# Routing by halves of a row and a first quad gathered from the token tiles, in a two-layer MoE trunk

## The chip, the cores and the metric

The kernel runs on one core of a Trainium2 chip. The metric is the device time of one execution, in microseconds (us); smaller is better. The engines are PE (TensorE, the matmul engine; PEld is its weight load), DVE (VectorE), ACT (ScalarE), POOL (GpSimd) and SP (SyncE, which here does nothing but issue the weight loads).

## What is computed

A decoder trunk of two layers on 528 tokens (16 meta tokens and 512 others) of 1024 columns, in float32. Each layer has a mixer (layer 0: a gated short convolution, layer 1: attention), an output projection added to the stream `h`, and a hierarchical mixture of experts (MoE). The MoE is what the change is about: 8 groups of 8 experts, each token goes to the group with the highest logit and there to two experts.

```python
def hier_moe(hn, w_grp, w_exp, w_gate, w_up, w_down):
    ...
    g_logits = (xf @ w_grp).astype(jnp.float32)
    p_grp = jax.nn.softmax(g_logits, axis=-1)
    grp = jnp.argmax(g_logits, axis=-1).astype(jnp.int32)
    ...
    e_in = jnp.einsum('ng,nge->ne', jax.nn.one_hot(grp, N_GROUPS, dtype=jnp.float32), e_logits)
    top_p, top_i = lax.top_k(jax.nn.softmax(e_in, axis=-1), TOP_K_IN_GROUP)
    gate = p_g * top_p / jnp.sum(top_p, axis=-1, keepdims=True)
    ...
    def expert_block(args):
        xb, e = args
        hh = jax.nn.silu(xb @ w_gate[e]) * (xb @ w_up[e])
        return hh @ w_down[e]
```

Here `hn` is the normalised stream (each row of `h` times its `rstd`, one over its root mean square, times a gain per column).

## The kernel before

**Tiles.** The tokens lie in four tiles of 128 rows, `h[0]` to `h[3]`, and in layer 0 a fifth of 16 rows, `hm` (index META). In layer 1 the meta tokens are gone and there are four tiles.

**Out-projection and routing.** `project_out` multiplies by the output weights in two halves of 512 columns. In each half the matmuls of all tiles (L292, three each for a split into a high and a low part) go into one PSUM bank per tile, `acc`, of which five are used in turn; as the last step of a half reaches a tile, VectorE adds its bank to `h` (L294). Only after the second half is `done(t)` called, which is `route(t)`: ScalarE squares and sums the row of 1024 columns, GpSimd makes `rstd`; TensorE transposes the tile in two lots of four (L372) through one PSUM bank, `tp`, ScalarE copies the first lot to `hT` (L375) and VectorE the second to `xT1` (L377); eight logit matmuls (L380) go into the PSUM bank `misc`, of which there is one, so the next tile's logits wait until this tile's have been read. Then a chain of some fourteen small VectorE instructions on 128x8 and 128x64 numbers finds the group and the two experts: `gm` (L383), `oh`, `mg`, `se` (L395), `s8`, `eq`, `gt`, `r8`, `M` (L403). `rank(t)` counts with a triangular matmul (L417) which place each token has in its expert and in its group: `rm` (L418), from it the one-hot `d` of places in group 0 (L419) and `aux` (L421); matmuls with ones (L422, L425) carry the counts to the tiles not yet ranked.

**First gather.** `first_gather` takes the tokens of group 0 out of the tiles: per tile one matmul for `aux` (L467) and two of 128x512 for `h` (L431), with `d` as the stationary operand; after the last tile VectorE copies `ag` (L473), ScalarE scales the gathered rows to `xg` (L436, two halves), VectorE makes `sel`, the places within the first four experts (L441), and TensorE selects and transposes them in one go, eight matmuls (L450) into two banks that VectorE multiplies by the gain into `xT0` and `xT1` (L451).

**Quads.** `run` then works through 16 quads of four experts: two `gate_up` passes (L589: all gate weights, then all up weights; PSUM bank `gu`), Silu and product, a transpose (L601), selection of the next quad's tokens, `down` (L621). Two quads share a group's gathered rows, so every second quad calls `gather(g)`: `d` for all tiles in one VectorE instruction, the `aux` matmuls (L561), the `h` matmuls (L431), `ag`, `xg`. In quad 0 the chain `gates` (L489 to L515) runs on VectorE and ScalarE beside the first matmuls, and five short matmuls (L744) after `down` fetch the gates of group 0.

**Order and buffers.** On TensorE the quads run in the order in which they are written. Out-projection and routing are ordered by the tile framework's scheduler, each engine getting a fixed list. The weights, 1 MB a tile, come in one fixed order through a ring of 22 buffers in the MoE stages (rings A, B and R). A load is issued (L101, SP) as soon as a buffer's last matmul is over, that is at the end of a `gate_up` pass or of `down`.

## Time and profile before

| | |
|---|---|
| median of three runs | 1403.22 us (1399.02, 1403.29, 1403.22) |
| profiled execution, its time | 1402.26 us |
| profiled execution, its span | 1400.5 us |
| mean granted TensorE clock | 0.958 |
| PE busy | 1245.6 us (89%) |
| DVE busy | 514.5 us (37%) |
| ACT busy | 310.4 us (22%) |
| weights and other data read | 434.40 MB |

The page cuts the span into 40 slices of 35 us, and gives for each the busy share of each engine in tenths, the granted TensorE clock and the share in which the 16 DMA engines move data. The busy share of TensorE is an average over stages with different limits, so stages are read one by one below: busy time by stretch, then single instructions in order of time. A line of a timeline is a run of like instructions on one engine; what stands in square brackets is the idle time before it and whose end ended that.

### The profile page before, as it was taken

How to read it: one execution, taken by the hardware profiler on the slowest of the kernel's cores; microseconds unless marked ns; L12 is line 12 of the kernel's file. 1: busy time of each engine (PE TensorE's matmuls, PEld its weight loads, DVE VectorE, ACT ScalarE, POOL GpSimd, SP SyncE). 2: the span in 40 equal slices, each digit the busy share in tenths (PEclk: the TensorE clock that was granted, in tenths of full speed). 3: DMA queues.
4: the chain of work that ended last, by engine and by line, in shares of the span. 5: the costliest groups of instructions: out<-in, count | busy, mean ns of one | idle time of the engine just before them, and what ended most of it. 6: DMA issues, size and time to landing. Idle time of an engine off the chain costs nothing.

```text
span 1400.5 us, 22937 instructions
## 1 busy us (share of the span) xinstructions
PE 1245.6 (89%) x9647; PEld 792.7 (57%) x9647; DVE 514.5 (37%) x1238; ACT 310.4 (22%) x708; POOL 58.6 (4%) x146
## 2 busy tenths in 40 slices
PE   8999999999889798878779999999997787888875
PEld 7999866545444343434378888875543334434432
DVE  5555336132131221423436676562230212113135
ACT  6333122011011010121044775331111010101112
POOL 2111101000000000000021000010000000000001
PEclk9999999999999999989989999999999999999998
DMA  7422563899999999999710012959999999999994
GB/s 282 151 91 91 211 249 151 367 420 419 420 419 419 420 420 419 419 421 421 306 42 28 30 63 84 367 219 382 420 420 420 420 419 420 420 419 420 420 418 168
DMA packets 65956, 438.13 MB, mean 313 GB/s; under 512 B 7457, under 2 KB 7841, under 8 KB 15282
## 3 DMA queue, kind: packets, MB, share of 16 engines
q1 hardware_dynamic: 64432, 434.74, 76.1%
q10 hardware_dynamic: 1154, 1.78, 0.4%
q8 instruction: 81, 1.33, 0.4%
q14 instruction: 33, 0.27, 0.1%
q0 software_dynamic: 256, 0.01, 0.0%
HBM read 434.40 MB, written 2.10 MB: 312 GB/s over the span
## 4 chain that ended last, share of the span: by engine, by line
DMA 26%; PE 20%; DVE 2%; ACT 1%; issue 1%; POOL 0%; DVEq 0%; ACTq 0%; SPq 0%; POOLq 0%
DMA R<-in_w_gate_dram 6%; DMA B<-in_w_down_dram 4%; DMA B<-in_w_up_dram 4%; DMA R<-in_w_up_dram 3%; DMA A<-in_w_up_dram 3%; PE gu L589 2%; PE a L1039 2%; PE sc L1202 2%; PE pj L1296 2%; PE acc L292 2%; DMA A<-in_w_gate_dram 1%; DMA A<-in_w_down_dram 1%; DMA R<-in_w_down_dram 1%; DMA B<-in_w_gate_dram 1%; PE pj L1182 1%; PE ot L1251 1%
## 5 line engine op out<-in xcount | busy, mean ns | idle before, releaser
L589 PE MATMUL gu<-R,xT 128*32 128x256 f32 x1856 | 161.1, 407 | 35.4 <-DMA R<-in_w_up_dram 22.9
L589 PE MATMUL gu<-B,xT 128*32 128x256 f32 x1376 | 149.4, 443 | 36.6 <-DMA B<-in_w_gate_dram 20.3
L589 PEld LDWEIGHTS gu<-R,xT 128*32 128x32 f32 x1856 | 78.4, 117 | 105.7 <-DMA R<-in_w_up_dram 30.8
L589 PEld LDWEIGHTS gu<-B,xT 128*32 128x32 f32 x1376 | 67.1, 126 | 97.8 <-issue 32.2
L589 PE MATMUL gu<-A,xT 128*32 128x256 f32 x720 | 96.6, 407 | 20.2 <-DMA A<-in_w_up_dram 13.3
L431 PE MATMUL w<-h,d 128*128 128x512 f32 x224 | 99.7, 598 | 0.0
L659 DVE TENSOR_TENSOR h<-h,w 128x512 f32<-128x512 f32 x144 | 89.5, 681 | 7.4 <-PE w L657 7.1
L562 DVE COPY ag<-w 128x18 f32<-128x18 f32 x14 | 2.5, 177 | 243.3 <-PE w L561 243.3
L596 ACT ACTIVATE sg<-gu 128x256 f32<-128x256 f32 x32 | 12.3, 384 | 337.6 <-PE gu L589 337.6
L657 PE MATMUL w<-yHL,d 128*128 128x512 f32 x288 | 83.4, 422 | 0.8 <-DVE h L659 0.5
L927 PE MATMUL acc<-xH,wH 128*128 128x264 f32 x384 | 79.9, 288 | 0.0
L631 ACT ACTIVATE y<-dn 128x512 f32<-128x512 f32 x60 | 35.8, 597 | 195.0 <-PE dn L621 187.8
L927 PE MATMUL acc<-xL,wH 128*128 128x264 f32 x384 | 79.0, 287 | 0.0
L927 PE MATMUL acc<-xH,wL 128*128 128x264 f32 x384 | 77.9, 284 | 0.0
L589 PEld LDWEIGHTS gu<-A,xT 128*32 128x32 f32 x720 | 44.0, 117 | 54.9 <-DMA A<-in_w_up_dram 17.6
L431 PEld LDWEIGHTS w<-h,d 128*128 128x128 f32 x224 | 41.4, 190 | 47.1 <-issue 46.4
L215 ACT ACTIVATE wH<-A,gc 128x256 fp32r<-128x256 f32 (+1 forms) x119 | 52.7, 520 | 61.2 <-PE acc L927 37.6
L450 PE MATMUL w<-sel,xg 128*128 128x128 f32 x480 | 61.6, 283 | 4.5 <-ACT xg L436 4.5
L621 PE MATMUL dn<-R,sg 128*32 128x512 f32 x472 | 63.7, 595 | 0.0
L657 PEld LDWEIGHTS w<-yHL,d 128*128 128x128 f32 x288 | 44.2, 178 | 33.1 <-DVE h L659 15.7
L450 PEld LDWEIGHTS w<-sel,xg 128*128 128x128 f32 x480 | 57.7, 197 | 7.2 <-ACT xg L436 7.2
L927 PEld LDWEIGHTS acc<-xL,wH 128*128 128x128 f32 x384 | 60.3, 189 | 0.0
(369 smaller groups left out, 2073.9 us busy)
## 6 DMA issues: line engine op xcount, KB each, us to landing
R<-in_w_up_dram SPq DMA_DIRECT2D x58, 1024.0 KB, 19.9
R<-in_w_down_dram SPq DMA_DIRECT2D x58, 1024.0 KB, 19.9
R<-in_w_gate_dram SPq DMA_DIRECT2D x58, 1024.0 KB, 19.9
B<-in_w_gate_dram SPq DMA_DIRECT2D x44, 1024.0 KB, 19.8
B<-in_w_up_dram SPq DMA_DIRECT2D x42, 1024.0 KB, 19.8
B<-in_w_down_dram SPq DMA_DIRECT2D x32, 1024.0 KB, 19.8
A<-in_w_down_dram SPq DMA_DIRECT2D x27, 1024.0 KB, 19.8
A<-in_w_gate_dram SPq DMA_DIRECT2D x26, 1024.0 KB, 19.9
```

The costliest lines, as they stand in the source:

```text
L215: i = A.activation(H, src, AF.Copy, scale=g)
L292: T.matmul(pt, l[:, j - base, c:c + n], r, start=j == first and m == 0, stop=j == last and m == 2)
L431: i = T.matmul(ps[u], d, h[t][:n, 512 * u:512 * u + 512], start=first, stop=last, skip_group_check=True)
L450: T.matmul(ps[:, k], self.xg[:, 4 * u + k], self.sel[q], start=True, stop=True)
L589: T.matmul(gu[CAP * e:CAP * e + CAP, s], xT[k // 4][:, k % 4, CAP * e:CAP * e + CAP], w[e][:, k], start=k == 0, stop=k == 7)
L621: T.matmul(dn[CAP * e:CAP * e + CAP, :n], hT[:, b, CAP * e:CAP * e + CAP], w[:, b, c:c + n], start=b == 0, stop=b == 1)
L631: A.activation(y[:, u], down_part(q, hT, u, 0, 512 * u, 512), AF.Copy)
L657: T.matmul(ps[:m, :n], DT[t], a, start=i == 0, stop=i == 1)
L659: V.tensor_tensor(hh, hh, ps[:m, :n], op=ALU.add)
L927: T.matmul(ps[:, u, :HALF], l[:, k, P * m:P * m + P], r[:, k, HALF * u:HALF * u + HALF], start=k == 0 and l is wH and r is xH, stop=k == 7 ...
L1039: T.matmul(a[:n, b, :c1 - c0], l[:, k, :n], r[:, k, c0:c1], start=k == 0 and m == 0, stop=k == 7 and m == 2)
L1202: T.matmul(ps[u][:, :w], l[:, q], r[:, w * u:w * u + w], start=m == 0, stop=m == 4 and u < nb - 1)
```

## The change

**Halves.** `done(t, half)` is called after each half. `route(t, u)` does for a half what can be done with it: the sum of squares (ScalarE, 512 columns), four transposes, the copy (ScalarE for half 0, VectorE for half 1) and four logit matmuls. All tiles' logits lie side by side in one bank. The chain from `gm` on and `rank` follow half 1. In layer 0, META comes behind tile 0 instead of ahead of it, and its folded sum uses the `tp` bank.

**First gather.** In place of `d`, `rank` makes `dr`, the one-hot of places in the first four experts (128 x 4 x 32), times `rstd`: two VectorE instructions, written into the memory of `xg`. `first_gather` multiplies eight column sets of each tile (`chunk8`: every eighth column, so the stationary operand is read with a step of 8 numbers) with `dr` straight into the two banks from which `xT0` and `xT1` are made. No `aux` matmul, `ag`, `xg` or selection stands ahead of quad 0.

**Quad 0.** After its two `gate_up` passes quad 0 now calls `gather(0)`, which gets the group's rows for quad 1, and the gates with them; the five L744 matmuls and their copy go.

```diff
@@ project_out
-        tiles = ((META,) if zM is not None else ()) + (0, 1, 2, 3)
+        tiles = (0,) + ((META,) if zM is not None else ()) + (1, 2, 3)
...
-                            pt = psum.tile([P, 512], F32, tag="misc", name="misc", bufs=1)
+                            pt = psum.tile([P, 512], F32, tag="tp", name="fold", bufs=1)
...
                         V.tensor_tensor(hh, hh, pt[:n], op=ALU.add)
-                        if half == 1:
-                            done(t)
+                        done(t, half)
@@ route
-        def route(self, t, psum):
+        def route(self, t, u, psum):
...
-            rstd_of(rp, rs, h[t][:n], n, D, junk=self.x0[0].rearrange("p k s -> p (k s)").bitcast(BF16))
-            hT = []
-            for u in range(2):
-                ps = psum.tile([P, 4, P], F32, tag="tp", name="tp", bufs=1)
-                for k in range(4):
-                    T.transpose(ps[:, k, :n], chunk(t, 4 * u + k), ident[:n, :n])
...
-            ps = psum.tile([P, 512], F32, tag="misc", name="misc", bufs=1)
-            for k in range(8):
-                T.matmul(ps[:n, :72], hT[k // 4][:, k % 4, :n], self.wg[:, k], start=k == 0, stop=k == 7)
+            rs, c = self.rstd[:n, t:t + 1], slice(512 * u, 512 * u + 512)
+            junk = self.x0[0].rearrange("p k s -> p (k s)").bitcast(BF16)
+            A.activation(junk[:n, :512], h[t][:n, c], AF.Square, accum_out=self.sq[:n, t, u:u + 1])
+            G.tensor_scalar(self.sq[:n, t, u:u + 1], self.sq[:n, t, u:u + 1], 1.0 / D, EPS if u == 0 else self.sq[:n, t, 0:1],
+                            op0=ALU.mult, op1=ALU.add)
+            ps = psum.tile([P, 4, P], F32, tag="tp", name="tp", bufs=1)
+            for k in range(4):
+                T.transpose(ps[:, k, :n], chunk(t, 4 * u + k), ident[:n, :n])
+            if u == 0:
+                hT = rp.tile([P, 4, P], F32, tag="hT", name="hT", bufs=1)
+                A.activation(hT[:, :, :n], ps[:, :, :n], AF.Copy)
+            else:
+                hT = self.x0[1]
+                V.tensor_copy(hT[:, :, :n], ps[:, :, :n])
+            if self.lg is None:
+                self.lg = psum.tile([P, 512], F32, tag="misc", name="misc", bufs=1)
...
+            ps = self.lg[:, 72 * t:72 * t + 72]
+            for k in range(4):
+                T.matmul(ps[:n], hT[:, k, :n], self.wg[:, 4 * u + k], start=u == 0 and t == 0 and k == 0, stop=u == 1 and k == 3,
+                         skip_group_check=True)
+            if u == 0:
+                return
+            G.tensor_tensor(rs, self.sq[:n, t, 1:2], nhalf[:n], op=ALU.pow)
...
+            if not self.done:
+                self.dr = self.xg.rearrange("p k s -> p (k s)")[:, :self.nT * P].rearrange("p (t s) -> p t s", t=self.nT)
@@ rank
-            V.tensor_scalar(self.d[:, t], iota(1, P), self.rm0[:, t, NE:NE + 1], None, op0=ALU.is_equal)
+            dr = self.dr[:, t]
+            V.tensor_tensor(dr.rearrange("p (e s) -> p e s", e=4), self.rm0[:, t, :4, None].to_broadcast([P, 4, CAP]),
+                            iota(1, CAP)[:, None, :].to_broadcast([P, 4, CAP]), op=ALU.is_equal)
+            V.tensor_scalar(dr, dr, self.rstd[:, t:t + 1], None, op0=ALU.mult)
@@ first_gather
-            ps, pa = [bank(), bank()], bank()
+            ps = [psum.tile([P, 512], F32, tag="acc", name="acc", bufs=5).rearrange("p (k s) -> p k s", k=4) for _ in range(2)]
             for t in self.done:
                 first, last = t == self.done[0], t == self.done[-1]
-                n = rows(t)
-                T.matmul(pa[:, :10], self.d[:n, t].bitcast(F32), self.aux[:n, t, :10], start=first, stop=last)
-                i = self.gather_tile(ps, t, first, last)
+                for u in range(2):
+                    for k in range(4):
+                        i = T.matmul(ps[u][:, k], chunk8(t, 4 * u + k), self.dr[:rows(t), t], start=first and k == 0, stop=last,
+                                     skip_group_check=True)
+                    if last:
+                        V.tensor_tensor(self.x0[u], ps[u], self.g8[:, 4 * u:4 * u + 4, None].to_broadcast([P, 4, P]), op=ALU.mult)
...
-            self.ag0 = self.new_ag()
-            V.tensor_copy(self.ag0[:, :10], pa[:, :10])
-            self.scaled_tokens(ps, self.ag0)
-            self.choose(0, self.ag0)
-            self.select(0, self.x0, bank)
@@ quad
-                        self.ag = self.ag0
+                        self.ag = gather(0)
+                        self.choose(0, self.ag)
...
-                        pa = bank()
-                        for t in tiles:
-                            n = rows(t)
-                            T.matmul(pa[:, :8], self.d[:n, t].bitcast(F32), self.aux[:n, t, 10:], start=t == 0, stop=t == nT - 1)
-                        V.tensor_copy(ag[:, 10:], pa[:, :8])
```

TensorE, layer 1, between the two halves of the out-projection. Before, tile 0's first routing stands within the second half (h_63 is tile 0, h_64 tile 1; oH and oL are the two parts of the attention output):

```order
L372 MATMUL tp<-cs,h_63 128x128 x4
L380 MATMUL misc<-wg,hT 128x72 x4
L292 MATMUL acc<-wL,oH 128x512
L292 MATMUL acc<-wH,oL 128x512
L380 MATMUL misc<-wg,xT_8815 128x72 x4
L372 MATMUL tp<-cs,h_64 128x128 x4
L292 MATMUL acc<-wH,oH 128x512
```

In the changed kernel these rows stand among the first matmuls of the second half:

```order
L386 MATMUL misc<-wg,hT 128x72 x4
L374 MATMUL tp<-cs,h_64 128x128 x4
L292 MATMUL acc<-wH,oL 128x512
L292 MATMUL acc<-wH,oH 128x512
L292 MATMUL acc<-wL,oH 128x512
L292 MATMUL acc<-wH,oL 128x512
L386 MATMUL misc<-wg,hT 128x72 x4
```

The transposes and logits of half 0, for every tile, have moved ahead of tile 0's second-half end.

TensorE, layer 1, from the last ranks to quad 0, before (h_66 is tile 3, A and R are weight tiles):

```order
L422 LDWEIGHTS one_b
L422 MATMUL rk<-M,one_b 128x64
L431 MATMUL acc<-h_66,d 128x512
L467 MATMUL acc<-aux,d 128x10
L431 MATMUL acc<-h_66,d 128x512
L450 MATMUL acc<-sel,xg 128x128 x8
L589 MATMUL gu<-A_8114,xT_8814 32x256
```

And in the changed kernel (L599 is the gate_up line, xg holds `dr`):

```order
L480 MATMUL acc<-xg,h_65 128x128 x2
L437 LDWEIGHTS one_b
L437 MATMUL rk<-M,one_b 128x64
L480 MATMUL acc<-xg,h_65 128x128
L480 MATMUL acc<-xg,h_66 128x128 x8
L599 MATMUL gu<-A_8148,xT_8848 32x256
```

The wide gather, the `aux` matmul and the selection are gone; one group of eight stands between the last ranks and quad 0.

VectorE, layer 1, the same place in the changed kernel, from `dr` of the last tile (L434) to the two products:

```order
L434 TENSOR_SCALAR xg<-xg,rstd 128x128
L499 TENSOR_REDUCE cm<-rk 128x8
L504 TENSOR_TENSOR ex<-gl,gm 128x32
L508 TENSOR_SCALAR o_6492<-r_8913 128x32
L500 TENSOR_SCALAR ov<-cm 128x8
L505 TENSOR_TENSOR ex<-ex,rstd 128x32
L509 TENSOR_SCALAR o_9445<-r_8913 128x32
L510 TENSOR_REDUCE m_9444<-s_8912 128x4
L523 TENSOR_TENSOR om<-oh,ov 128x32
L566 TENSOR_TENSOR d<-rm_6495,cs 128x512
L483 TENSOR_TENSOR xT_8848<-acc,g_75 128x512
L483 TENSOR_TENSOR xT_8849<-acc,g_75 128x512
```

Eight instructions of `gates` and the `d` of `gather(0)` stand ahead of the products.

TensorE, layer 0, quad 0 behind its up pass, before:

```order
L589 MATMUL gu<-R_1868,xT_125 32x256
L589 MATMUL gu<-R_1870,xT_125 32x256
L601 MATMUL w<-cs,sg 128x128 x2
L450 MATMUL w<-sel,xg 128x128 x8
L621 MATMUL dn<-R_1872,sg 32x512
```

And in the changed kernel:

```order
L599 MATMUL gu<-R_1870,xT_125 32x256
L571 MATMUL w<-aux,d 128x18 x5
L446 MATMUL w<-h_63,d 128x512 x2
L446 MATMUL w<-h_64,d 128x512 x2
L446 MATMUL w<-h_65,d 128x512 x2
L446 MATMUL w<-h_66,d 128x512 x2
L446 MATMUL w<-hm,d 128x512 x2
L611 MATMUL w<-cs,sg 128x128 x2
L465 MATMUL w<-sel,xg 128x128 x8
L631 MATMUL dn<-R_1872,sg 32x512
```

The group's gather has moved in between the up pass and the down-projection.

## Rows read from the trace of the kernel before

**Rows 1.** Stretches summed: length, busy us by engine (count), PEclk, DMA share, GB/s.

```profile
245.00:248.00 3.00, 3.00 (x64) 1.80 (x60) 0.02 (x1) 0.00 (x0) 0.00 (x0) 1.00 0.00 0
250.00:680.00 430.00, 377.20 (x3125) 185.35 (x3117) 115.11 (x240) 53.11 (x106) 0.00 (x0) 0.94 1.01 419
...
949.00:1370.00 421.00, 358.53 (x3065) 177.61 (x3058) 97.75 (x204) 45.46 (x90) 0.00 (x0) 0.95 1.01 419
```

**Rows 2.** Loads on the SyncE queue by time: start us, us taken, line, tile.

```profile
247.90 0.80 SPq L101 DMA_DIRECT2D R<-in_w_down_dram  x2
248.80 3.36 SPq L101 DMA_DIRECT2D R<-in_w_gate_dram  x4
252.26 0.87 SPq L101 DMA_DIRECT2D R<-in_w_up_dram  x2
...
946.85 1.11 SPq L101 DMA_DIRECT2D A<-in_w_down_dram  x2
```

**Rows 3.** TensorE by time, first quads: start us, us, line, out<-in, [idle before].

```profile
244.22 7.11 PE L589 MATMUL gu<-R,xT 128*32 128x256 f32 x128
...
258.17 1.37 PE L744 MATMUL w<-aux,d 128*128 128x8 f32 x10
...
943.18 0.41 PE L589 MATMUL gu<-A,xT 128*32 128x256 f32 x2 [0.78 <-DVE xT L451]
```

**Rows 4.** VectorE by time, layer 1, last ranks to quad 0.

```profile
936.75 0.23 DVE L418 SCALAR_TENSOR_TENSOR rm<-rk,M 128x72 f32<-128x72 f32 x1 [0.30 <-PE rk L417]
937.02 0.29 DVE L419 TENSOR_SCALAR d<-cs,rm 128x128 fp32r<-128x128 f32 x1
...
941.54 0.69 DVE L451 TENSOR_TENSOR xT<-acc,g 128x512 f32<-128x512 f32 x1 [0.18 <-PE acc L450]
```

**Rows 5.** TensorE by time, layer 1, the last tile's gather and the selection.

```profile
937.36 1.12 PE L431 MATMUL acc<-h,d 128*128 128x512 f32 x2
...
940.35 2.05 PE L450 MATMUL acc<-sel,xg 128*128 128x128 f32 x16 [0.78 <-ACT xg L436]
```

**Rows 6.** VectorE by time, layer 0, tile 0's second-half add and the last ranks.

```profile
207.95 0.69 DVE L294 TENSOR_TENSOR h<-h,acc 128x512 f32<-128x512 f32 x1 [0.22 <-PE acc L292]
...
238.65 0.23 DVE L418 SCALAR_TENSOR_TENSOR rm<-rk,M 128x72 f32<-128x72 f32 x1 [0.30 <-PE rk L417]
```

**Rows 7.** VectorE by time, layer 1, tile 0's add, and one tile's turn.

```profile
914.09 0.69 DVE L294 TENSOR_TENSOR h<-h,acc 128x512 f32<-128x512 f32 x1 [6.12 <-PE acc L292]
...
928.64 0.17 DVE L383 TENSOR_REDUCE gm<-misc 128x1 f32<-128x8 f32 x1 [0.17 <-PE misc L380]
...
933.06 0.23 DVE L418 SCALAR_TENSOR_TENSOR rm<-rk,M 128x72 f32<-128x72 f32 x1 [0.92 <-PE rk L417]
...
933.71 0.16 DVE L383 TENSOR_REDUCE gm<-misc 128x1 f32<-128x8 f32 x1
```

**Rows 8.** TensorE by time, layer 1, a half's routing, the out-projection's last matmul.

```profile
915.29 0.67 PE L372 MATMUL tp<-cs,h 128*128 128x128 f32 x4
...
916.61 0.48 PE L292 MATMUL acc<-wL,oH 128*128 128x512 f32 x1
...
924.01 0.39 PE L292 MATMUL acc<-wH,oL 128*128 128x512 f32 x1
```

**Rows 9.** Stretches summed, layer 0: the stretch with the lowered clock.

```profile
224.00:232.00 8.00, 8.00 (x35) 5.61 (x35) 3.74 (x16) 0.76 (x3) 0.00 (x0) 0.58 1.01 428
```

**Rows 10.** TensorE by time, layer 0: the out-projection's end; quad 1's gather and after.

```profile
218.40 0.39 PE L292 MATMUL acc<-wH,zL 128*128 128x512 f32 x1
...
269.82 1.39 PE L561 MATMUL w<-aux,d 128*128 128x18 f32 x10
...
286.46 0.83 PE L589 MATMUL gu<-R,xT 128*32 128x256 f32 x12
```

**Rows 11.** Groups by line and shape, TensorE's weight loads | busy us, mean ns.

```profile
L450 PEld LDWEIGHTS w<-sel,xg 128*128 128x128 f32 x480 | 57.7, 197 | 7.2 <-ACT xg L436 7.2
...
L372 PEld LDWEIGHTS tp<-cs,h 128*128 128x128 f32 x64 | 10.1, 210 | 3.2 <-ACT hT L375 1.7 <-issue 0.8 <-ACT M L388 0.2
```

More of the change, by code (lines that the diff above doesn't have):

```diff
@@ L355, in prepare @@
             self.r8 = rp.tile([P, nT, 8], F32, name="r8", bufs=1)
+            self.sq = rp.tile([P, nT, 2], F32, name="sq", bufs=1)
+            self.lg = None
             self.done = []
@@ L361, in prepare @@
                 G.memset(self.rstd[:, META:], 1.0)
-        def route(self, t, psum):
+        def route(self, t, u, psum):
             rp, n = self.rp, rows(t)
-            rs = self.rstd[:n, t:t + 1]
-            rstd_of(rp, rs, h[t][:n], n, D, junk=self.x0[0].rearrange("p k s -> p (k s)").bitcast(BF16))
-            hT = []
-            for u in range(2):
-                ps = psum.tile([P, 4, P], F32, tag="tp", name="tp", bufs=1)
-                for k in range(4):
-                    T.transpose(ps[:, k, :n], chunk(t, 4 * u + k), ident[:n, :n])
-                hT.append(rp.tile([P, 4, P], F32, tag="hT", name="hT", bufs=1) if u == 0 else self.x0[1])
-                if u == 0:
-                    A.activation(hT[u][:, :, :n], ps[:, :, :n], AF.Copy)
-                else:
-                    V.tensor_copy(hT[u][:, :, :n], ps[:, :, :n])
-            ps = psum.tile([P, 512], F32, tag="misc", name="misc", bufs=1)
-            for k in range(8):
-                T.matmul(ps[:n, :72], hT[k // 4][:, k % 4, :n], self.wg[:, k], start=k == 0, stop=k == 7)
+            rs, c = self.rstd[:n, t:t + 1], slice(512 * u, 512 * u + 512)
[14 more added lines that the diff above has]
+                self.lg = psum.tile([P, 512], F32, tag="misc", name="misc", bufs=1)
+                assert n == P
+            ps = self.lg[:, 72 * t:72 * t + 72]
[5 more added lines that the diff above has]
+            G.tensor_tensor(rs, self.sq[:n, t, 1:2], nhalf[:n], op=ALU.pow)
@@ L457, in first_gather @@
         def first_gather(self, psum):
-            def bank():
-                return psum.tile([P, 512], F32, tag="acc", name="acc", bufs=5)
             self.sel = {}
-            ps, pa = [bank(), bank()], bank()
+            ps = [psum.tile([P, 512], F32, tag="acc", name="acc", bufs=5).rearrange("p (k s) -> p k s", k=4) for _ in range(2)]
             for t in self.done:
                 first, last = t == self.done[0], t == self.done[-1]
-                n = rows(t)
-                T.matmul(pa[:, :10], self.d[:n, t].bitcast(F32), self.aux[:n, t, :10], start=first, stop=last)
-                i = self.gather_tile(ps, t, first, last)
+                for u in range(2):
[4 more added lines that the diff above has]
+                        V.tensor_tensor(self.x0[u], ps[u], self.g8[:, 4 * u:4 * u + 4, None].to_broadcast([P, 4, P]), op=ALU.mult)
                 if t == self.done[-3]:
@@ L953, in trunk_kernel @@
         project_out(lambda j: [wp.tile([P, 512], F32R, tag=a, name=a) for a in ("wH", "wL")], psum, "out", zH, zL, zM, STEPS[0],
-                    lambda t: moe0.route(t, psum))
+                    lambda t, u: moe0.route(t, u, psum))
         moe0.first_gather(psum)
@@ L1317, in part @@
         return [w[:, 512 * (j - 4):512 * (j - 3)] for w in whole]
-    project_out(part, psum, "o", *oT[1], None, STEPS[1], lambda t: moe1.route(t, psum))
+    project_out(part, psum, "o", *oT[1], None, STEPS[1], lambda t, u: moe1.route(t, u, psum))
     moe1.first_gather(psum)
```

## The prediction

> **What bounds the kernel now.** I read the stretches summed first. In both MoE stages the DMA engines are full: a share of 1.01 at 419 GB/s over 430 us of layer 0 and over 421 us of layer 1 [rows 1]. TensorE is busy for 377 of the 430 us there, so in these stages it waits for weights, not the other way round. A load is 1024 KB, which at 419 GB/s is 2.5 us. Ahead of each full stretch the stream stands still: share 0.00 from 245 to 248 us [rows 1]. All ring buffers are full and nothing is released until quad 0 has used its gate weights. The SyncE queue shows it: its first load after the pause goes out at 247.90 in layer 0, 3.68 us after the first gate_up matmul at 244.22, and in layer 1 at 946.85, 3.67 us after 943.18 [rows 2, 3]. So the time from the start of quad 0 (call it G) to the end of each layer is a fixed amount of weights at a fixed rate, and each microsecond by which G comes earlier is a microsecond off the end, once per layer, as long as the stream never runs dry afterwards. The sum is therefore two shifts of G, less any dry spell.
>
> **Where G comes from, layer 1 first.** The last ranks of the last tile start at 936.75 and G follows 6.43 us later [rows 3, 4]: d, the wide gather (937.36), ag, xg, the selection (940.35, 2.05 us), the products [rows 4, 5]. In layer 0 the same tail is 238.65 to 244.22, 5.57 us [rows 3, 6].
>
> *The new tail.* TensorE: ranks to d 0.27, one more VectorE instruction of the same kind 0.27, hand-over as from d to the gather 0.34 (937.02 to 937.36), then four of the eight matmuls, priced as the selection, whose product began 1.19 us after it (940.35 to 941.54) [rows 4, 5]: 2.07 us. VectorE has to get through aux and dr, eight instructions of gates and a 128x512 d ahead of the product (the order shows them): 0.54 for ranks and dr, and by estimate 0.4 for aux and the scaling, 0.1 each for eight small ones that overlap (one lasts 0.16 to 0.23 [rows 7]) and 0.6 for d (a 128x512 product lasts 0.69): 2.35 us. The later of the two counts, 2.35, then the product 0.69 and a hand-over 0.1: 3.15 us. In layer 1 the first gate_up matmul of before waited for the second product (0.78 idle, released by xT L451) [rows 3], which would make it 3.8. The gate bank there is the third of the five acc banks; the thirteenth request of before, the selection's second half, held it, while after ten requests of the changed kernel its last holder is tile 3 of the out-projection, long read. I take 3.15 and keep 3.8 for the range. The tail shrinks by 3.3 us in layer 1 and 2.4 in layer 0.
>
> *When the last ranks come.* Routing of half 0 moves ahead of tile 0's second half. Four transposes and their logits take 1.32 us (915.29 to 916.61) [rows 8]; TensorE has no gap there, so four tiles delay tile 0's add from 914.09 [rows 7] by 5.3 to 919.4. None of it is new work; what is left behind each tile is halved, and the limit becomes VectorE. One turn of a tile on it, gm to gm, is 5.07 us with 0.92 of waiting [rows 7]; that turn holds one aux and d pair too many (0.4), and gets the tile's own add (0.6) and the second dr instruction (0.2): 4.55 us, an estimate. Four turns less what follows the last ranks (0.85): 919.4 + 18.2 - 0.85 = 936.75, the same as before, if the 0.92 wait is filled by the next tile's work, as the order allows. Is TensorE then late? It leaves the out-projection at 924.4 plus the two halves that it has done more by then (2.6), 927.0 [rows 8]; four tile gathers at 2.05 [rows 5] and about 3.1 of transposes, logits and ranks end at 938.3, and G could be 938.2 by it, against 936.75 + 3.15 = 939.9 by VectorE. TensorE has 1.7 us to spare. **G falls from 943.18 to 939.9, a gain of 3.3 us**; bounds 0 (the 0.92 waits all stay) and 4.5 (VectorE packs tighter by 0.3 a turn).
>
> **Layer 0.** Tile 0's add moves from 207.95 [rows 6] by 5.3 and by META's first half (about 1.0), less META's folding and second half, which now come behind it (about 1.0): 213.3. Four turns of 4.55 and META's, whose small instructions are as many, about 4.0, less 0.85: 234.6. META's narrow steps leave waits that nothing fills: between none and five times 0.92, I take half, 2.3: 236.9. G = 236.9 + 3.15 = 240.0, against 244.22: **a gain of 4.2 us**, bounds 2 and 6.5. It is more than in layer 1 because before lost time here to the clock: from 224 to 232 us the granted clock was 0.58 of full, so mostly at 1.2 in place of 2.4 GHz, with TensorE busy for all 8.00 us [rows 9]. It fell while the engine did transposes, logits and META's 16-row matmuls. The changed kernel has more of the same short work there and no 512-column gather. If the clock falls again, 0.42 x 8 = 3.4 us of TensorE's work is lost; its own path ends some 4 us ahead of VectorE's (out-projection to 218.8 [rows 10] and 2.6 more as in layer 1, five gathers of 2.05, 4 us of the rest: 235.7), but the loss meets single hand-overs too, so I price it at 2 us, between 0 and 3.4.
>
> The Trainium skill (TensorE: Matmul & The Clock Gate, section What's actually happening) says that the clock is set by how busy the engine has been. The trace agrees that it moves without any change in the program, but not that a full busy share holds it: 8.00 of 8.00 us at 0.58. By the page alone the new idle gaps of TensorE there would bring the fall, and the sum would be that of rival B.
>
> **Quad 0.** The gather of group 0 moves behind the up pass. In quad 1, which does the same, aux matmuls, gather, xg, selection and down-projection take from 269.82 to 286.46, 16.64 us [rows 10]. So down's buffers come free 7.11 + 16.64 = 23.8 us after G, in place of 13.95 (L744 at 258.17, right behind down) [rows 3]. Until then the stream lives on the eight loads that the two passes release (2 + 4 + 2 by 258) [rows 2]: 8 x 2.5 = 20 us from about G + 5 (rates are full by 250 at the latest [rows 1]), to G + 25. A load issued at 23.8 moves data 1.2 to 2.1 us later (247.90 to full by 250). Dry for 0 to 0.9 us in layer 0; I take 0.5. In layer 1 there is no META gather (2 us less) and none is dry. Later releases have a margin, since from there on TensorE waits for weights. The removed L744 (1.37) is in the 16.64 already. `gates` needs the aux numbers only by the first aux matmul at G + 7.1, and in before it was done ahead of G, so nothing queues behind it. The xg copies stand ahead of Silu on ScalarE, inside the 16.64.
>
> **Other edits.** Two Squares of 512 in place of one of 1024 and one more small GpSimd instruction a tile: both engines have room (0.76 and 0.00 of 8 us in the stretch from 224 to 232 [rows 9]), so I take nothing for them. In layer 0 the half-0 Squares and copies stand between weight splits on ScalarE; at worst a TensorE gap at the half boundary, which no row prices; three instructions of the 128x512 size (0.69 [rows 4]) would be 2 us, and I take 0. The loads that SyncE issues at the out-projection's end come some 3 us later; their weights are used only in the up pass.
>
> **Sum.** 3.3 + 4.2 - 0.5 = 7.0 us off the profiled execution: 1402.26 - 7.0 = 1395.3. That execution lies 1 us under the median of the three runs.
>
> **The rivals.**
> A, the forecast: 1395.3, from 1391 to 1398.5.
> B, the clock falls in layer 0 as before: gain 3.3 + 2.2 - 0.5 = 5.0, 1397.3, up to 1400 with more lost in quad 0. For it: the same kind of work ran at 0.58 [rows 9]. Against it: layer 1.
> C, **slower**: the stationary operand with a step of 8 numbers loads at half the rate. No row has that step. Transposes, which load with a step of 2, took 210 ns a load, the selection's packed ones 197 [rows 11], 7% more; nearest to that, a step of 8 costs little, and 1.7 us of TensorE's slack hide up to a fifth. Doubling decides from about there: four gathers cost 8.2 us more in layer 1, 938.2 + 8.2 = 946.4 (+3.2); in layer 0 five cost 10.3, 235.7 + 10.3 = 246 (+1.8). With the dry spell +5.5: 1407.8.
> The Trainium skill (SBUF — State Buffer, section Door 1: The DMA port swizzle) says that memory lines are 16 bytes and that every access that crosses to a new line pays a penalty, so that up to 4 float32 may be strode over for free. By it each number of these loads, 32 bytes apart, pays, and the result is C; it gives no size for it, and the traced step of 2 lies within a line.
> D, the halves buy nothing on VectorE: its turns keep the 0.92 wait (G 943 in layer 1, 242.3 in layer 0): gain 0 + 1.9 - 0.5, 1401.
> E, quad 0's gather starves the stream: any delay of down beyond 23.8 is lost in full; half the clock over a third of the 16.64 us costs 5.5 in layer 0 and, with 2 us of margin, 3.5 in layer 1: up to 1404.
>
> **How the numbers follow.** Chances: A 0.42, B 0.20, C 0.16, D 0.14, E 0.08. The predicted time is A's, 1395. The range holds A, B, D and most of E, 1391 to 1405, and leaves C and tails out. Three tenths of a per cent, about what a measurement of this kernel can tell from no change, is 4.2 us on 1403.22: faster means under 1399.0. That is A (0.40 of it), most of B (0.13): 0.53. Within: D, E, the rest of B and A: 0.31. Slower, over 1407.4: C mostly, 0.16.
>
> **What would show it.** Right: first gate_up matmul near 240 and 940; last ranks of layer 1 near 936.8 with VectorE nearly gapless from 919; loads again 3.7 us after G; eight-matmul gathers in 2.05 us. Wrong: gathers near 4 us (C); a granted clock near 0.5 between 222 and 240 (B); gaps of 0.9 us ahead of the ranks on VectorE (D); a share well under 1 around G + 25 (E).

## The result, and the profile after

The changed kernel takes 1410.91 us (median; 1408.6 to 1414.98), the kernel before 1403.22 (five runs of each): the ratio is 1.0064, 95% interval 1.0048 to 1.008. It is slower by 0.6%, where 1395 was forecast, and above the range of 1391 to 1405. The profiled execution took 1408.6 us, with a span of 1406.8.

TensorE by time in the changed kernel, layer 1, from the next-to-last ranks to quad 0 (start us, us, line, out<-in, count, [idle before]; L480 is the new first gather, xg holds `dr`; the program's eight 128x128 matmuls of a tile show as x16):

```profile
940.84 0.20 PE L429 MATMUL rk<-M,tri_b 128*128 128x72 bf16 x1
...
942.13 2.65 PE L480 MATMUL acc<-xg,h 128*128 128x128 f32 x10
944.61 0.20 PE L429 MATMUL rk<-M,tri_b 128*128 128x72 bf16 x1
944.64 1.19 PE L480 MATMUL acc<-xg,h 128*128 128x128 f32 x4
945.67 0.19 PE L437 MATMUL rk<-M,one_b 128*128 128x64 bf16 x1
945.70 4.53 PE L480 MATMUL acc<-xg,h 128*128 128x128 f32 x18
950.16 0.41 PE L599 MATMUL gu<-A,xT 128*32 128x256 f32 x2
```

No row has an idle time: TensorE is full to the end, and its groups are long. In layer 0 the last tile's group stands alone:

```profile
246.77 4.07 PE L480 MATMUL acc<-xg,h 128*128 128x128 f32 x16
250.77 1.50 PE L599 MATMUL gu<-R,xT 128*32 128x256 f32 x24
```

4.07 us for 16, where the selection took 2.05 [rows 5]. VectorE, which was to set the pace, waits for it, in layer 1 ahead of each of the last three `rm` and of the products:

```profile
941.07 0.23 DVE L430 SCALAR_TENSOR_TENSOR rm<-rk,M 128x72 f32<-128x72 f32 x1 [1.66 <-PE rk L429]
...
944.85 0.23 DVE L430 SCALAR_TENSOR_TENSOR rm<-rk,M 128x72 f32<-128x72 f32 x1 [1.59 <-PE rk L429]
...
948.36 0.69 DVE L483 TENSOR_TENSOR xT<-acc,g 128x512 f32<-128x512 f32 x1 [0.99 <-PE acc L480]
```

The reason is one level lower, in the weight loads. One line's loads in layer 1: count, ns least/median/most, first and last start:

```profile
L480 PEld LDWEIGHTS acc<-xg,h x64: 312/335/340, 932.7 to 949.7; 128*128 128x128 f32 x64
```

335 ns (the median) in place of 197 on average for the packed ones [rows 11]. G, the start of quad 0, is 250.77 in layer 0 (244.22 before) and 950.16 in layer 1 (943.18 before). SyncE's first loads after the pause:

```profile
254.44 0.80 SPq L101 DMA_DIRECT2D R<-in_w_down_dram  x2
...
953.83 1.11 SPq L101 DMA_DIRECT2D A<-in_w_down_dram  x2
```

Both are 3.67 us after G, as in [rows 2, 3]. Stretches summed (length, busy us PE, PEld, DVE, ACT, POOL, granted clock, DMA share, GB/s), to be laid beside [rows 1, 9]:

```profile
234.00:242.00 8.00, 8.00 (x37) 7.42 (x37) 3.58 (x21) 0.59 (x3) 0.00 (x0) 0.50 0.15 61
242.00:244.00 2.00, 2.00 (x11) 1.92 (x11) 1.86 (x10) 0.18 (x1) 0.00 (x0) 0.60 0.01 4
926.00:930.00 4.00, 3.85 (x24) 3.04 (x24) 3.66 (x17) 1.11 (x4) 1.91 (x6) 1.00 0.00 0
930.00:934.00 4.00, 3.29 (x22) 2.96 (x22) 3.38 (x18) 1.00 (x4) 1.02 (x3) 0.89 0.71 268
934.00:938.00 4.00, 3.93 (x25) 3.79 (x24) 1.89 (x11) 0.39 (x2) 0.00 (x0) 0.69 1.01 426
276.00:278.00 2.00, 2.00 (x39) 1.01 (x38) 0.70 (x4) 0.00 (x0) 0.00 (x0) 1.00 0.89 344
257.00:680.00 423.00, 378.38 (x3092) 186.56 (x3081) 115.04 (x242) 54.42 (x108) 0.00 (x0) 0.96 1.01 419
957.00:1378.00 421.00, 364.72 (x3068) 180.74 (x3061) 98.42 (x207) 46.96 (x93) 0.00 (x0) 0.95 1.01 419
```

The stages are saturated again, the dry spell in quad 0 is 0.2 us (a share of 0.89 over 2 us), and the clock falls to the 1.2 GHz level in layer 0 for some ten microseconds, and for some three in layer 1 too.

In layer 1 the time is best read from the first out-projection matmul, which starts at another time in each execution (896.07 before, 898.07 after): G follows 47.11 us later before, and 52.09 after. Three effects lie in that: the halves, the new gather, and its step of 8.

### The profile page after: what moved, and what is told of

Same layout as the page of the kernel before. It is cut to its first block, busy times and chain, and to the rows that moved or that the text cites. A ratio compares the mean times of both kernels' runs of the same rounds, so it can differ in the third digit from the quotient of the medians.

```text
span 1406.8 us, 23178 instructions
## 1 busy us (share of the span) xinstructions
PE 1268.7 (90%) x9741; PEld 818.3 (58%) x9741; DVE 518.5 (37%) x1247; ACT 313.9 (22%) x726; POOL 56.7 (4%) x155
## 5 line engine op out<-in xcount | busy, mean ns | idle before, releaser
L599 PE MATMUL gu<-R,xT 128*32 128x256 f32 x1856 | 157.0, 405 | 24.8 <-DMA R<-in_w_up_dram 13.6
L599 PE MATMUL gu<-B,xT 128*32 128x256 f32 x1376 | 141.5, 428 | 32.7 <-DMA B<-in_w_gate_dram 17.0
L599 PEld LDWEIGHTS gu<-R,xT 128*32 128x32 f32 x1856 | 76.6, 116 | 90.3 <-issue 24.6
L599 PE MATMUL gu<-A,xT 128*32 128x256 f32 x720 | 101.4, 426 | 22.9 <-DMA A<-in_w_up_dram 13.9
L599 PEld LDWEIGHTS gu<-B,xT 128*32 128x32 f32 x1376 | 64.9, 122 | 90.3 <-issue 26.6
L446 PE MATMUL w<-h,d 128*128 128x512 f32 x256 | 114.0, 598 | 0.0
L599 PEld LDWEIGHTS gu<-A,xT 128*32 128x32 f32 x720 | 46.0, 121 | 61.7 <-DMA A<-in_w_up_dram 18.2
L446 PEld LDWEIGHTS w<-h,d 128*128 128x128 f32 x256 | 47.4, 190 | 53.8 <-issue 53.1
```

Of the source, the lines that this page charges most:

```text
L446: i = T.matmul(ps[u], d, h[t][:n, 512 * u:512 * u + 512], start=first, stop=last, skip_group_check=True)
L599: T.matmul(gu[CAP * e:CAP * e + CAP, s], xT[k // 4][:, k % 4, CAP * e:CAP * e + CAP], w[e][:, k], start=k == 0, stop=k == 7)
```

## The experiments

Totals are medians, each ratio is against the kernel before as it ran beside that kernel, and G is read from the profiled execution; "wait to G" is the time in layer 1 from the first out-projection matmul to G.

| kernel | routing | first gather | total us (ratio, interval) | G, layer 0 | wait to G |
|---|---|---|---|---|---|
| before | rows | wide | 1402 to 1403 | 244.22 | 47.11 |
| changed | halves | step 8 | 1410.91 (1.0064, 1.0048 to 1.008) | 250.77 | 52.09 |
| e1_packed | halves | packed | 2439.47, not comparable | 244.42 | 45.23 |
| e2_step2 | halves | step 2 | 1399.13 (0.9973, 0.996 to 0.9987) | 243.55 | 45.45 |
| e3_step4 | halves | step 4 | 2453.13 (one run), not comparable | 250.67 | 51.80 |
| e4_halves | halves | wide | 1411.41 (1.0062, 1.0046 to 1.0079) | 254.08 | 49.57 |
| e5_gather | rows | step 2 | 1396.98 (0.9957, 0.9942 to 0.9972) | 244.31 | 43.88 |
| e7_logits_first | halves | step 2, late | 1407.85 (1.0041, 1.0026 to 1.0056) | 249.83 | 48.41 |
| e8_meta_first | halves | step 2, late | 1407.05 (1.0034, 1.002 to 1.0048) | 248.78 | 48.72 |
| e9_meta_late | rows | step 2 | **1391.51** (0.9932, 0.9918 to 0.9945) | 238.56 | 43.84 |
| e10_no_meta | rows | step 2 | 1387.78 (one run) | 237.51 | 43.87 |
| e11_step8_whole_rows | rows | step 8 | 1410.62 (1.0053, 1.0039 to 1.0067) | 252.44 | 50.06 |
| e12_halves_meta_late | halves | step 2 | 1400.60 (0.9985, 0.9975 to 0.9995) | 245.49 | 45.45 |
| e13_before_meta_late | rows | wide | 1399.73 (0.9981, 0.9971 to 0.9991) | 240.85 | 47.14 |

### The step of the stationary operand

Three kernels differ from the changed one in the columns that a load takes. With a step of 1 or 4 the columns meet other weight rows, so tokens route differently later on and only the time up to G is to be read; the thousand microseconds that both totals have more lie behind layer 1's G (942.00 in e1_packed, 953.20 in e3_step4). With a step of 2 quad 0's gate and up weights are laid out to match, and all is computed.

```diff
-  T.matmul(ps[u][:, k], chunk8(t, 4 * u + k), self.dr[:rows(t), t], ...)
+  e1: h[t][:rows(t), 512 * u + 128 * k : 512 * u + 128 * k + 128]
+  e3: h[t][:rows(t), 512 * u : 512 * u + 512].rearrange("r (p b) -> r b p", b=4)[:, k]
+  e2: chunk(t, 4 * u + k)          # every second column
```

> The changed kernel, with the first gather's stationary operand read in one piece (128 columns side by side) in place of every eighth column; the columns then meet the wrong weight rows, so this part of the result is not the reference's. All four engines keep their order. G is the first gate_up matmul, counted in layer 1 from the first out-projection matmul: 47.1 us in the kernel before, 52.1 in the changed one. Theory S (the step of 8 numbers slows the weight load, 335 in place of 192 ns, and eight matmuls take 4.07 in place of 2.05 us): load back to about 192 ns, eight matmuls in 2.05, G in layer 1 at 43.8 to 45, total 1394 to 1399. Rival H (the halves themselves put TensorE behind): eight matmuls in 2.05 but G at 50 or later, total 1407 or more. Rival K (the fall of the granted clock in layer 0, 0.50 from 234 to 242 us, is what costs): layer 1 as in S, the clock falls again in layer 0 and half of the loss stays, total 1400 to 1404.

> The changed kernel, with the first gather's stationary operand read with a step of 4 numbers (16 bytes); columns meet the wrong weight rows, so that part of the result is not the reference's. Orders unchanged. Theory S as a matter of 16-byte lines with a step of 4 still free: weight load 192 to 215 ns, eight matmuls in 2.05 us. Theory S as a cost of every new line: load about 335 ns as with a step of 8. A cost that grows with the step: between, 250 to 280 ns.

> The changed kernel, with the first gather's stationary operand read with a step of 2 numbers, and quad 0's gate and up weights laid out to match (2 KB pieces in place of 8 KB, 8 loads a layer, which come while the stream is not full); the whole computation is there. Theory S: load 195 to 210 ns (transposes with that step 209), eight matmuls in 2.05 to 2.2, G in layer 1 44 to 45 after the out-projection's first matmul, total 1394 to 1399, so faster than before by 0.3 to 0.6%. Rival H: as the changed kernel, 1407 or more. If the 2 KB pieces matter, quad 0 waits for weights in its first pass.

Loads of the new gather, packed, step 4, step 2 (the last in layer 1 alone):

```profile
L480 PEld LDWEIGHTS acc<-xg,h x128: 186/192/338, 225.3 to 941.7; 128*128 128x128 f32 x128
```

```profile
L480 PEld LDWEIGHTS acc<-xg,h x128: 308/331/335, 224.7 to 952.8; 128*128 128x128 f32 x128
```

```profile
L483 PEld LDWEIGHTS acc<-xg,h x64: 194/196/198, 928.8 to 939.3; 128*128 128x128 f32 x64
```

A step of 2 loads like packed data, a step of 4 like one of 8. Layer 1's wait to G follows: 45.23, 45.45, 51.80, 52.09. The step alone is worth 6.6 us of G there, and the total falls from 1410.91 to 1399.13. The new layout of the weights isn't what does it: e1_packed has the old one and the same wait within 0.2 us. So theory S holds, and of the three forms that e3_step4's expectation gives it the one in which every new line costs, though e1_packed and e2_step2 end just behind S's bounds (45 for the wait, 1399 for the total). The packed loads of 338 ns are those under the lowered clock; the step of 8 hides there. In the changed kernel half a tile's gather (x8) took 2.11 us at the full clock and 2.19 in the stretch at 0.50:

```profile
226.89 2.11 PE L480 MATMUL acc<-xg,h 128*128 128x128 f32 x8
...
239.28 2.19 PE L480 MATMUL acc<-xg,h 128*128 128x128 f32 x8
```

The Trainium skill (SBUF — State Buffer, Door 1: The DMA port swizzle) asks for two hits in a 16-byte line and goes on that a stride of 4 float32 is free. The first half agrees with these rows (a step of 2 hits a line twice), the second doesn't: a step of 4 cost 331 ns.

### The halves alone, the gather alone

e4_halves has routing by halves, with the first gather and quad 0 as before. e5_gather has the new gather (step of 2) and `gather(0)` in quad 0, with routing of whole rows as before:

```diff
 e4   def rank(self, t): ...          # d, aux as before
 e4   def first_gather(self, psum): ... # wide gather, ag, xg, selection as before
 e5 -   def route(self, t, u, psum):
 e5 +   def route(self, t, psum):      # whole rows, META first, as before
```

> Only the halves: routing by halves as in the changed kernel, first gather and quad 0 as before. Theory S: the halves alone neither help nor hurt much, since the long tail stays (6.4 us from the last ranks in layer 1) and VectorE sets the pace: G in layer 1 46 to 48, total 1400 to 1405. Rival H: G 50 or later in layer 1, total 1407 or more.

> Only the other part: first gather from the tiles with a step of 2 and the group's gather inside quad 0, but whole rows routed after the second half as in the kernel before. Theory P (packed loads are worth the shorter tail, and the halves cost by themselves, since they hold tile 0's add back by 5 us): G in layer 1 at 43.5 to 45 after the out-projection's first matmul, G in layer 0 near 241.5, total 1394 to 1398, that is no later than with the halves. Rival Q (halves and gather need each other: the gain comes only when the halves have taken work off each tile's turn): G in layer 1 at 46 or later, total 1401 or more.

The halves alone lose 9 us, the gather alone gains over 5. Of e4_halves' expectation the total is rival H's (1407 or more), and the wait of 49.57 is above theory S's 46 to 48 and just short of H's 50; e5_gather is theory P's in layer 1 and in the total, while its G in layer 0, 244.31, is 3 us later than expected. Most of e4_halves' loss lies in layer 0, where G comes 9.86 us later than before and the clock is down for longer than in [rows 9]:

```profile
234.00:238.00 4.00, 3.67 (x10) 1.63 (x10) 2.31 (x12) 0.39 (x2) 0.00 (x0) 0.50 0.40 168
...
246.00:250.00 4.00, 3.56 (x8) 1.75 (x7) 2.23 (x16) 0.53 (x2) 0.00 (x0) 0.50 0.00 0
```

How much of that is the clock and how much the halves themselves wasn't separated. In layer 1, where the clock of both stays at 1.00, the halves cost 2.46 (49.57 against 47.11) and the gather gains 3.23 (43.88). VectorE of e2_step2 (halves) in layer 1, its first out-projection matmul at 894.17, shows why; it holds tile 0's add, then the last ranks:

```profile
918.27 0.69 DVE L297 TENSOR_TENSOR h<-h,acc 128x512 f32<-128x512 f32 x1 [8.61 <-PE acc L295]
...
936.53 0.23 DVE L433 SCALAR_TENSOR_TENSOR rm<-rk,M 128x72 f32<-128x72 f32 x1 [0.40 <-PE rk L432]
```

And the same two of e5_gather (whole rows; first matmul at 895.60):

```profile
913.62 0.69 DVE L297 TENSOR_TENSOR h<-h,acc 128x512 f32<-128x512 f32 x1 [6.12 <-PE acc L295]
...
936.39 0.23 DVE L425 SCALAR_TENSOR_TENSOR rm<-rk,M 128x72 f32<-128x72 f32 x1 [0.34 <-PE rk L424]
```

From the add to the last ranks it is 18.26 us with halves and 22.77 without: the turns do become shorter, by 4.5. But the add comes 24.10 after the first matmul in place of 18.02, 6.1 later. The balance is 1.6 us lost, in a layer with an undisturbed clock.

### TensorE's order

Does the order on TensorE spoil the halves? In e7_logits_first no tile is gathered before all logits are through; e8_meta_first also puts META first in the second half.

```diff
+  with behind(*([self.logits] if first else [])):   # e7: last logit matmul
       i = T.matmul(ps[u][:, k], chunk(t, 4 * u + k), ...)
+  if half == 1: tiles = (META, 0, 1, 2, 3)          # e8, besides
```

> Halves and gather with a step of 2, and every logit matmul placed ahead of the first gather's matmuls on TensorE. Theory O (TensorE's fixed order is what is left of the miss: gather groups stand ahead of logits for which VectorE waits, 0.5 to 1.6 us a tile in layer 0): G in layer 1 at 43.5 to 44.5, in layer 0 240 to 242, total 1394 to 1397. Rival K (the fall of the clock to half in layer 0 is what is left): layer 1 as now, 45.4, G in layer 0 243 to 245, total 1398 to 1401; TensorE idles more between the logits, so the clock may fall earlier.

> As the one with all logits first, and META ahead of tile 0 in the second half (half 0 unchanged). Theory O: META's narrow chain then runs while VectorE waits for the out-projection, about 2 us less in layer 0, G in layer 0 238 to 240, layer 1 unchanged, total 1392 to 1396. Rival K: G in layer 0 as without this edit, within 1 us.

Both are worse than e2_step2. e7_logits_first is later than theory O and rival K had it (K's totals end at 1401), and e8_meta_first has its G in layer 0 one microsecond earlier than that, as K allows. Stretch 226 to 236 of e7_logits_first, the end of its layer 0 on TensorE, and on VectorE the last tile's `gm` and the last ranks:

```profile
226.00:236.00 10.00, 5.91 (x33) 4.82 (x33) 7.75 (x42) 1.38 (x8) 1.03 (x3) 0.64 1.02 430
```

```profile
242.22 3.69 PE L484 MATMUL acc<-xg,h 128*128 128x128 f32 x16
...
246.36 3.54 PE L484 MATMUL acc<-xg,h 128*128 128x128 f32 x28
```

```profile
237.28 0.17 DVE L396 TENSOR_REDUCE gm<-misc 128x1 f32<-128x8 f32 x1 [1.32 <-PE misc L389]
...
245.98 0.23 DVE L433 SCALAR_TENSOR_TENSOR rm<-rk,M 128x72 f32<-128x72 f32 x1 [4.48 <-PE rk L432]
```

TensorE stands idle for 4.1 of 10 us between the short steps, then has all gathers ahead of it at the end. The gathers had been filling waits that were there anyway: with no gather ahead of it, the last tile's `gm` follows tile 0's add by 22.05 us (215.23 to 237.28), in e2_step2 by 22.08 (214.07 to 236.15), and now the last ranks wait 4.48 us for TensorE. So this order doesn't help, and nothing here shows the gathers pushing the logits back. It isn't a clean test: the clock was down for longer, 0.50 from 230 to 238, and in layer 1, where e2_step2 holds 1.00, from 932 to 938.

### The step without the halves

e11_step8_whole_rows is e5_gather with `chunk8` for `chunk` and the weights as in the changed kernel.

> The changed kernel with routing of whole rows as before, so that only the first gather (step of 8) and quad 0 differ from the kernel before; e5_gather is the same with a step of 2. Theory C (the price is in the step: 335 ns a load in place of 209, a tile's gather 4.05 in place of 2.05 to 2.8 us): 4 gathers in layer 1 add up to 5 to 8 us to 43.9, of which what lies beside VectorE's turns is hidden: 48 to 51; layer 0 with a fifth (META's) and the clock at half: 248 to 252; total 1405 to 1411, so most of the loss of the changed kernel with no halves in it. Rival H (the step costs as much only where the halves leave TensorE no gap): 45 to 46 in layer 1, total under 1401.

1410.62 us against 1396.98, 13.6 us for the step alone; the wait to G is 50.06 against 43.88, as theory C has it. And the changed kernel, 1410.91, adds the halves and ends at the same total, though its own wait to G is 52.09: in layer 0 the clock of e11_step8_whole_rows is at 0.50 from 226 to 242, about twice as long as in the changed kernel, and its G there is 252.44 against 250.77.

### The clock in layer 0

In e5_gather TensorE has no gap from 206 us to G, its clock falls in 224 to 226 and stays at 0.50 to 238. META's eight gather matmuls have 16 rows each and stand ahead of the other tiles'. e9_meta_late moves them behind tile 2's, e10_no_meta drops them, e13 and e12 do the move in the kernel before and in e2_step2.

```diff
-  for t in self.done:
-      first, last = t == self.done[0], t == self.done[-1]
+  order = [0, 1, 2] + ([META] if META in self.done else []) + [3]
+  for t in order:
+      first, last = t == order[0], t == order[-1]
```

> The kernel of e5_gather, with META's 16 matmuls of the first gather (16 rows each) placed behind tile 2's in place of ahead of tile 0's; nothing else differs. In e5_gather they start at 221.1 us in layer 0 and the granted clock is 0.69 at 224-226 and 0.50 from 226 to 238, with TensorE busy all the time. Theory K (the clock falls on META's 16-row matmuls): the fall comes with them, so later and shorter; the stretch 224 to 232 is at 0.9 or more, G in layer 0 comes at 240 to 241.5, total 1393 to 1394. Rival L (the clock falls on the run of transposes, 72-column logits and short gathers of all tiles, whatever META does): 0.50 over some 10 us as before, G at 243.5 to 245, total within 2 us of 1397. Layer 1 has no META: 43.9 from the first out-projection matmul to G by both.

> The kernel of e9_meta_late without META's matmuls in the first gather: the 16 meta tokens are missing from quad 0 of layer 0, the rest is computed. 16 matmuls that take 3.2 us in e5_gather go. Theory K: the clock stays at 0.9 or more from 220 to 244 us and G in layer 0 falls by 3.2 us of work and by about 6 us (12 us at 0.50 in place of 1.00), though VectorE's turns then hold it: 236 to 238. Rival L: the clock falls to 0.50 for 8 us or more all the same, G falls by the work alone: 240 to 242. Layer 1 unchanged, 43.9.

> The kernel before with META's four 16-row matmuls of the first gather (and their aux matmuls) behind tile 2's, nothing else. Theory K: the granted clock, 0.58 from 224 to 232 us in the kernel before, stays at 0.95 or more; 3.4 us of TensorE's work come back, of which some lies beside VectorE's turns: G in layer 0 at 241 to 242.5 in place of 244.22, total 1399 to 1400.5. Rival L (the clock falls on the transposes and 72-column logits, whatever META does): 0.58 as before, G at 243.5 to 245, total 1401 to 1403. Layer 1 stays at 47.1.

> The kernel of e2_step2 (halves, step of 2) with META's 16 matmuls of the first gather behind tile 2's. Theory K (the clock falls on META's 16-row matmuls): the granted clock stays at 0.95 or more from 226 to 244 us, where e2_step2 has 0.91, 0.50 and 0.74 in 232 to 238; about 5 us at half the clock go, 2.5 to 3 us: G in layer 0 at 240.5 to 241. Theory P (the halves cost in themselves): layer 1 stays at 45.4 from the first out-projection matmul to G, layer 0 stays 2 us behind e9_meta_late's 238.56, total 1395.5 to 1397. Rival Q (with the clock held the halves catch up): G at 238.6 or less in layer 0, total within 2 us of e9_meta_late's 1391.5.

Four stretches of e5_gather, then of e9_meta_late, and one of e13_before_meta_late:

```profile
218.00:222.00 4.00, 4.00 (x30) 3.50 (x28) 2.86 (x13) 2.73 (x7) 1.83 (x6) 1.00 0.58 197
222.00:226.00 4.00, 4.00 (x28) 3.58 (x28) 2.68 (x12) 0.39 (x2) 0.00 (x0) 0.85 1.01 426
226.00:230.00 4.00, 4.00 (x18) 3.38 (x18) 0.86 (x6) 0.69 (x2) 0.00 (x0) 0.50 1.01 426
...
234.00:238.00 4.00, 4.00 (x21) 3.94 (x21) 0.91 (x7) 0.00 (x0) 0.00 (x0) 0.50 0.00 0
```

```profile
218.00:222.00 4.00, 3.37 (x29) 2.94 (x28) 2.97 (x15) 2.36 (x7) 1.83 (x6) 1.00 0.68 233
222.00:226.00 4.00, 4.00 (x36) 3.92 (x35) 3.02 (x16) 0.71 (x3) 0.00 (x0) 1.00 1.02 430
226.00:230.00 4.00, 4.00 (x37) 3.87 (x36) 2.91 (x16) 0.55 (x3) 0.00 (x0) 1.00 1.01 426
...
234.00:238.00 4.00, 4.00 (x32) 3.64 (x30) 3.09 (x17) 0.24 (x1) 0.00 (x0) 1.00 0.00 0
```

```profile
226.00:230.00 4.00, 4.00 (x29) 3.20 (x29) 3.34 (x15) 0.76 (x3) 0.00 (x0) 1.00 1.01 426
```

From 222 us on the busy share in these stretches is the same, with up to twice as many matmuls. G comes 5.75 us earlier, more than theory K asks, and the total is 1391.51, the fastest kernel here that leaves nothing out. e13_before_meta_late shows the same in the kernel before: [rows 9] has 0.58 there, it holds 1.00, and G falls by 3.4 us. e10_no_meta gains one more microsecond of G (237.51): what META's matmuls cost in themselves is little. One more thing differs, though: without META's matmuls to fill it, TensorE idles for 0.63 us between 218 and 222 in e9_meta_late and e10_no_meta, and for 0.82 in e13_before_meta_late. Such a gap isn't enough, since in e2_step2 and e12_halves_meta_late 0.9 us of idle time between 222 and 226 came ahead of a fall; but the two weren't separated.

But the rule isn't "16 rows lower the clock". In e9_meta_late these matmuls run at 234 to 236, at 1.00:

```profile
234.08 0.73 PE L476 MATMUL acc<-xg,hm 16*128 16x128 f32 x4
...
234.88 1.68 PE L476 MATMUL acc<-xg,hm 16*128 16x128 f32 x12
```

And in e12_halves_meta_late, against its expectation, the clock falls all the same, with META's gather still to come (at 241.33), and G is 245.49:

```profile
230.00:234.00 4.00, 2.19 (x16) 1.84 (x16) 3.43 (x19) 0.39 (x2) 0.00 (x0) 0.84 1.01 426
234.00:238.00 4.00, 4.00 (x21) 3.94 (x21) 1.28 (x9) 0.21 (x1) 0.00 (x0) 0.50 0.42 176
```

There TensorE had been idle for 1.8 of 4 us before. So the clock fell once after a full stretch with narrow matmuls in it, once after a stretch with gaps. The Trainium skill (TensorE: Matmul & The Clock Gate, What's actually happening) has the clock follow how busy the engine has been: that fits the second fall and not the first. In kernels with whole rows META's place decides, whether by its rows or by the gap that it leaves; with halves it doesn't, and what does stays open. Against e9_meta_late the halves lose 9.1 us: 1.6 in layer 1, and 6.9 of G in layer 0, where the clock is in it.

## Why the prediction was wrong

**The step that failed: the price of a tile's gather.** The prediction took 2.05 us from the packed selection, weighed the load "nearest to" the transposes' step of 2 and wrote that "a step of 8 costs little". It cost 4.03 to 4.07. That is rival C, held at 0.16: its mechanism and its sign were right, and its row was named (gathers near 4 us). The nearest row was on the wrong side of the edge; what the Trainium skill says of 16-byte lines (SBUF — State Buffer, Door 1: The DMA port swizzle) had it closer, without a size. By e11_step8_whole_rows against e5_gather that step is 13.6 us of the total, by e2_step2 against the changed kernel 11.8.

**C itself was undersized.** That its 1407.8 lies close to the profiled 1408.6 is luck: its shifts of G, 3.2 and 1.8, make 5.0, where 4.98 and 6.55 make 11.5, and 4.55 came back between the layers, which no sum had (below). In layer 1 its TensorE sum put G 50.33 after the first out-projection matmul (946.4 - 896.07); it was 52.09. The out-projection's last matmul started 31.39 after the first, 3.45 later than before [rows 8], where the sum allowed 2.6, and TensorE has 0.86 us of gaps from 926 to 934 (busy 3.85 and 3.29 of 4): 1.7 of the 1.8. The lowered clock there isn't it: e3_step4 holds 1.00 and has 51.80. In layer 0 the sum gave 246, and G was 250.77. There the clock does cost: one half's logits (x8) take 1.01 us at 226 and 1.82 at 237, while the gathers take as long as at full clock:

```profile
226.04 1.01 PE L386 MATMUL misc<-wg,xT 128*128 128x72 f32 x8
...
237.66 1.82 PE L386 MATMUL misc<-wg,xT 128*128 128x72 f32 x8
```

The 4.8 us weren't taken apart further. C and B were priced as if one excluded the other; they came together, and since the step hides the clock they don't add.

**The halves.** "None of it is new work ... and the limit becomes VectorE" is half right. With the step out of the way (e2_step2, layer 1) VectorE's stretch from tile 0's add to the last ranks was 18.26, forecast 17.35; the add came 24.10 after the first matmul, forecast 23.3. The forecast let the two cancel; they miss it by 1.7. Neither the forecast nor rival D had the case in which the halves cost. In layer 0 the forecast's last ranks, 236.9, came at 245.76 in the changed kernel and at 240.38 in e2_step2.

**What held.** The tail: forecast 3.15; 3.09 in layer 1 of e2_step2 and e5_gather (936.39 to 939.48), 5.31 in the changed kernel. The first gate_up matmul didn't wait for the second product: it stands at 950.16, the product starts at 950.27. Layer 1's gain of 3.3, as a gain of the gather alone: e5_gather's 43.88 is the forecast's 43.8 (939.9 - 896.07), by the tail, not by the halves. Loads go out 3.67 us after G. Quad 0's dry spell was 0.2 us, forecast 0.5, and rival E's starved stream isn't seen in the changed kernel (share 1.01 from 257 to 680 us). In layer 1 a shift of G goes through to the end: from its G to the end of the span it is 457.3 us before, 456.6 after, 456.8 in e9_meta_late. Layer 0's forecast of 240.0 was reached in no kernel with halves (e2_step2, the best, has 243.55); e9_meta_late's 238.56 comes from whole rows and a clock that holds, so it doesn't bear the forecast out.

**What the sum left out.** The two shifts, 6.55 and 4.98, make 11.5, yet the profiled execution grew by 6.3 in its span. 4.55 came back between the layers: from layer 0's G to layer 1's first out-projection matmul it is 651.85 us before and 647.30 after, and in the nine other kernels that compute everything 647.1 to 651.5. It wasn't forecast, and its cause stays open. The clock goes with it: from 432 to 436 us after layer 0's G it is 0.62 before and 1.00 after, and from 456 to 472 us after it 0.68 and 0.79; how much of the 4.55 that makes wasn't measured.

## What to carry to other kernels

Before a stationary operand is read with a step, time that very step: fp32 columns two apart loaded like packed ones, four apart cost 70% more, and a layout of the weights that keeps the step at two took 11.8 us off. Work that is moved ahead of a critical step on a full engine isn't free: in layer 1 it held tile 0's add back by 6.1 us and shortened what followed by 4.5, so count both. When TensorE is full through a stretch of short matmuls, read its granted clock in slices and try another place for the narrowest ones: here that was worth 5.5 us (1396.98 to 1391.51) with whole rows, and nothing with halves (1399.13 to 1400.60).

## What was not expected of the hardware

A load with a step of 4 or 8 numbers took 331 to 336 ns (medians) at either level of the clock, a packed one 192 at 2.4 GHz and 333 at 1.2: the step costs as much as the lowered clock, and the two don't add. The changed kernel's own, first at 0.50, then at 1.00:

```profile
L480 PEld LDWEIGHTS acc<-xg,h x14: 312/336/338, 239.2 to 242.8; 128*128 128x128 f32 x14
...
L480 PEld LDWEIGHTS acc<-xg,h x23: 312/334/336, 244.7 to 250.3; 128*128 128x128 f32 x23
```

The packed ones of e1_packed at 0.50, and the stretch that they stand in:

```profile
L480 PEld LDWEIGHTS acc<-xg,h x11: 333/333/338, 233.9 to 237.7; 128*128 128x128 f32 x11
```

```profile
234.00:238.00 4.00, 4.00 (x20) 4.00 (x20) 1.66 (x11) 0.25 (x2) 0.00 (x0) 0.50 0.47 199
```

And between the out-projection and quad 0 of layer 0 the clock fell to 1.2 GHz in every kernel but those with whole rows and META late or left out, in some of them (the kernel before, e5_gather, e11_step8_whole_rows) with TensorE busy without a gap.
